# PSUM banks held through the expert stage, skipped parts without zeros, and a nested condition

## The chip, the cores and the metric

The kernel runs on one core of one Trainium2 chip. The metric is the device time of one execution in microseconds (us). Engines are named as in the profile: PE is TensorE (matmuls), PEld its weight loads, DVE is VectorE, ACT is ScalarE, POOL is GpSimd, SP is SyncE, which issues most DMAs. PSUM is the accumulation memory that PE writes and DVE and ACT read; the kernel uses it as eight banks of 128 partitions by 512 float32.

## What is computed

The reference is a two-layer diffusion backbone over 256 latent tokens and 256 context tokens of 1024 features. Each layer mixes tokens (gated linear attention and grouped-query attention in layer 0, Mamba-2 and Fourier mixing in layer 1) and then runs a mixture of 16 experts, of which each token uses two. The change touches only that second half:

```
s = sigmoid(h @ router_w)                      # the two best experts of the best group of four
idx, w = route(h, router_w, router_b)          # w: the two gates, normalised to sum 1
for each expert e, over the tokens x on its list:
    y = (silu(x @ w_gate[e]) * (x @ w_up[e])) @ w_down[e]
    out[token] += gate * y
x = layer_norm(alpha * x + m5 * out)
```

Layer 0 has 512 tokens (context and latent), layer 1 only the 256 latent ones. How many tokens an expert gets is known only at run time.

## The kernel before

The program is straight-line code for each engine; a scheduler with a cost model orders the instructions of each engine when the kernel is built, and semaphores join the engines. In layer 0 the expert stage runs from about 380 to 862 us of the profiled execution, in layer 1 from about 1080 to 1508 us.

*A list in four parts.* The list of an expert has 128 slots, in four parts of 32: part t holds slots 32 t to 32 t + 31. Experts are taken in pairs (members m = 0, even, and m = 1, odd). A part that no token falls into is skipped at run time: `when(rv, least, yes, no)` reads the expert's count from a register and, on PE, compares it with 32, 64 or 96 and branches. Where a part is skipped, the Else branch runs `z_mm` instead: one bf16 matmul of a 128 x 128 tile of zeros (`zero`) that writes zeros over the bank, so that those who read it find numbers. Not every condition has an Else: the combine's second half and the last condition of the down product add to a bank that is already written.

*The steps of a pair*, with the names that the profile uses (0p and 1p stand for the two layers):
- `lists` (sl): the token numbers and gates of the slots, by a matmul of a one-hot matrix G; DVE then copies them out of PSUM into tg, sp, tok and gt (L1508 to L1519). One pair's lists are made while the pair before is computed.
- `features` (xt): the tokens of the slots, features across partitions, in halves S = 0 and S = 1 of 64 slots per member. In layer 0 by an indirect DMA and PE transposes, in layer 1 by a matmul with G. Each half fills two banks, evacuated by ACT. S = 1 is conditional (count over 64).
- `hidden` (gu): gate and up products of the four parts, each in a bank, and `swiglu` by ACT (sg) and DVE (h). Parts 2 and 3 are two conditions, one behind the other.
- `down` (dp): two banks, S = 0 for parts 0 and 1, S = 1 for parts 2 and 3; for S = 1 the product of part 3 stands first with an Else, then that of part 2 without. ACT and DVE take the bank out as y (L316, L1655).
- `combine` (cm): a matmul with one-hot rows adds the pair's outputs at their tokens, and DVE adds the banks to the accumulator, called big (L1562). It runs inside the next pair's odd expert.

*Banks.* `ps(name, tag)` takes a fresh tile out of a pool with three tags: pj (two banks), a (two) and b (four). Each request is a tile of its own, and the pool hands it a bank of its tag as one becomes free in the order that the scheduler settles on. sl, xt and the odd expert's dp use a; the gate and up parts use pj (parts 2 and 3 of even experts b); cm and the even expert's dp use b.

*Helpers.* Every matmul has the line of `mm`, L340, every PE transpose that of `tr`, L345, every condition L1460, and every ACT function L316, so the profile is read by tile names. The weights stream through slots in loads of 1.5 MB on SP's queue.

Of the kernel before, what the change touches and what calls it, by code (L numbers as in the profile page):

```python
# [10 lines left out]
BF16 = mybir.dt.bfloat16  # L11
# [3 lines left out]
OP = mybir.AluOpType  # L15
# [19 lines left out]
# weight slots in the areas while the experts run  # L35
# [3 lines left out]
# ---------------------------------------------------------------- host layout  # L39
# [13 lines left out]
# parameters and constants: '' for the whole run, 'A' and 'B' for the mixers of the two layers  # L53
# [79 lines left out]
def host_layout(a):  # L133
# [41 lines left out]
    # (layer, third, k, half, p, 1024): sixteen units per third, in loads of three and one  # L175
# [19 lines left out]
    # (l, e, k quarter, p, k, tile, gate or up, feature): each tile holds a quarter of the features  # L195
# [3 lines left out]
    # (l, e, half, p, b, output): the partitions hold the b-th 32 features of each quarter  # L199
# [34 lines left out]
# ---------------------------------------------------------------- kernel  # L234

# the column groups of a weight matrix, each loaded where it is first used and kept until it is dropped
# [19 lines left out]
# generators, each a step at a time  # L256
# [6 lines left out]
# pieces of one tile  # L263
# [11 lines left out]
class Core:  # L275
    def __init__(self, tc, I, O, dbg=None, stop=None):
        self.tc, self.nc, self.I, self.O = tc, tc.nc, I, O
        self.dbg, self.stop = dbg or {}, stop
        self.table, self.acts = None, []
        self.held = set()  # L280
        self.pin = False

# [19 lines left out]
    # the four 16 KB areas b, o, a, x hold whatever lives across the parts of a layer  # L302
# [8 lines left out]
    def ps(self, name, tag='a'):  # L311
        return self.psp.tile([128, 512], F32, tag=tag, bufs={'pj': 2, 'a': 2, 'b': 4}[tag], name=name)

    # activations: a table set asked for is loaded behind those that need the one before, and before those that need it
# [62 lines left out]
    # between the layers: LayerNorm, and the modulated input of layer 1  # L377
# [29 lines left out]
    # out = x * exp(-ln(1 + exp(-x))); t is scratch  # L407
# [6 lines left out]
    # a third of layer l's adaLN rows for both streams, as per-partition scalars mods[l][:, m, kt, stream]  # L414
# [57 lines left out]
    # acc = alpha * x + m2 * (o @ w_o); LayerNorm; v = modulated x for the experts; acc = alpha * x  # L472
# [31 lines left out]
    # layer 1's acc = alpha * x + m2 * (o @ w_o), over the features A of o, there before the others, and then B;  # L504
    # of the first N outputs all of A first
# [71 lines left out]
    # out = modulated, and x = alpha * (affine) of the normalized x, the stream h of acc  # L577
# [17 lines left out]
    # rows 0, 1: scale and offset of modulate(n * g + b); rows 2, 3: those of alpha * (n * g + b)  # L595
# [11 lines left out]
    # x (128, KT, n) <- (x - mean) / sqrt(var + eps) over the features, in place  # L607
# [32 lines left out]
    # a stream's LayerNorm, in parts of n tokens, each followed by what is done with it  # L640
# [18 lines left out]
    # scratch of normalize  # L659
# [9 lines left out]
    # x (in place) and its two parts, exact in float32r, of the modulated input  # L669
# [15 lines left out]
    # a weight chunk in two parts  # L685
# [8 lines left out]
    # x in two parts, exact in float32r  # L694
# [9 lines left out]
    # a product of two operands in parts: all but that of the two low parts, which is below float32's accuracy  # L704
# [7 lines left out]
    def even_mixer(self, uT, u, W):  # L712
# [6 lines left out]
        # low-rank decay inputs: partial sums over k on four column tiles  # L719
# [41 lines left out]
        # scratch: the places of the gated linear attention's later results, and the input's  # L761
# [35 lines left out]
    def attention(self, oT, gk, gv):  # L797
        nc, pt = self.nc, self.pt
        # the keys in two parts: the high one of each kv head on both halves of the partitions, the low one where the keys are
# [13 lines left out]
    # 1 / sqrt(scale * x + eps): exp(-ln / 2) and one Newton step y * (1.5 - (scale * x + eps) * y * y / 2)  # L813
# [38 lines left out]
    def gla_states(self, i, q, k_, v, dec, mem):  # L852
# [3 lines left out]
        for di in range(2):  # L856
# [17 lines left out]
            # att[(cp, m), pair, l] = sum_d ke[d, m] qe[d, l], then its causal half  # L874
# [35 lines left out]
    def gla_heads(self, i, S, v, oT, mem):  # L910
        nc = self.nc
        for hh in range(2):
# [14 lines left out]
            # RMS norm over the value features  # L927
# [20 lines left out]
    # heads i (partitions 0-63, kv 0) and i + 4 (partitions 64-127, kv 1)  # L948
    def attend(self, q, k, v, oT, i, strm):
# [4 lines left out]
        # a head's queries in two parts, the high one where they are, the low one on the other half of the partitions  # L954
# [41 lines left out]
    # ------------------------------------------------------------ layer 1 mixer  # L996
# [21 lines left out]
    def odd_mixer(self, uT, parts):  # L1018
# [3 lines left out]
        # by streams: of the context's, nothing is needed once the states are there  # L1022
# [7 lines left out]
        # dt rows: heads of direction 0 at partitions 0-11, of direction 1 at 32-43  # L1030
# [19 lines left out]
        with tc.tile_pool(name='mixB1', bufs=1) as p1:  # L1050
# [17 lines left out]
            # token-major x and b, where the input was  # L1068
# [26 lines left out]
    def dt_tables(self, lr):  # L1095
# [28 lines left out]
        # weights of the tokens in their chunk's final state: dt * exp(sum of the later log decays)  # L1124
# [12 lines left out]
        # decay over the first latent chunk of each direction, on every partition  # L1137
# [38 lines left out]
    def ssd_heads(self, xb, xt, cs, HS, tabs, zs, oT, middle, last):  # L1176
# [4 lines left out]
        # the decays in two parts, exact in float32r, and what picks the rows of both  # L1181
# [266 lines left out]
    def experts(self, l, nb, pm, rows, xg, zero, pos, number, aux):  # L1448
# [4 lines left out]
        def z_mm(p, n):  # L1453
            self.mm(p[:, :n], zero, zero.unsqueeze(1).broadcast_to([128, n // 128, 128]))

        def when(rv, least, yes, no=None):
# [3 lines left out]
            with tc.If(rv > least) as cmp:  # L1460
                yes()
# [305 lines left out]
```

## Time and profile before

| | |
|---|---|
| device time, three runs | 1543.07, 1537.3, 1539.64 us; median 1539.64 |
| span of the profiled execution | 1528.9 us |
| own time of the profiled execution | not listed apart; the median of the runs is 10.7 us above its span |
| PE, DVE, ACT busy | 1298.6, 755.5, 417.4 us |
| mean DMA rate | 260 GB/s |

The span is the time from the first to the last instruction in the trace, the device time also holds what lies around it. "Busy" counts the time in which an engine executes something; matmuls overlap each other, so counts and starts say more about PE than a sum of durations. In an order of events a row is a run of like instructions of one engine: its start, the time to its end, and the count; in square brackets stands how long the engine was idle before it and what it waited for. "issue" means that the engine waited for nothing that the profile shows, "PEq" that PE's own sequencer (branches and semaphores) held it.

### The profile page before, as it was taken

How to read it: one execution, taken by the hardware profiler on the slowest of the kernel's cores; microseconds unless marked ns; L12 is line 12 of the kernel's file. 1: busy time of each engine (PE TensorE's matmuls, PEld its weight loads, DVE VectorE, ACT ScalarE, POOL GpSimd, SP SyncE). 2: the span in 40 equal slices, each digit the busy share in tenths (PEclk: the TensorE clock that was granted, in tenths of full speed). 3: DMA queues.
4: the chain of work that ended last, by engine and by line, in shares of the span. 5: the costliest groups of instructions: out<-in, count | busy, mean ns of one | idle time of the engine just before them, and what ended most of it. 6: DMA issues, size and time to landing. Idle time of an engine off the chain costs nothing. (4 is left out here: it accounts for less than half of the span.)

```text
span 1528.9 us, 28267 instructions
## 1 busy us (share of the span) xinstructions
PE 1298.6 (85%) x11753; PEld 799.5 (52%) x11754; DVE 755.5 (49%) x1899; ACT 417.4 (27%) x831; POOL 66.1 (4%) x68
## 2 busy tenths in 40 slices
PE   3999987996889889999988779989696778987774
PEld 0787643684334454665445348858442455544433
DVE  2756447776426233233344487567541544344534
ACT  3533243452112111111111243444321211121213
POOL 0000002011000000000000030030100000000000
PEclk8999988998899999999999989999898999999876
DMA  9322666044678978779987222652788998999931
GB/s 388 121 93 83 247 249 262 0 172 173 271 304 339 398 300 332 321 293 383 387 359 293 111 85 83 223 204 100 313 321 342 378 373 354 387 375 416 410 129 30
DMA packets 43700, 397.60 MB, mean 260 GB/s; under 512 B 4976, under 2 KB 9200, under 8 KB 12272
## 3 DMA queue, kind: packets, MB, share of 16 engines
q1 hardware_dynamic: 41200, 388.40, 63.1%
q0 software_dynamic: 1728, 4.20, 0.8%
q8 instruction: 158, 2.59, 0.7%
q10 hardware_dynamic: 576, 2.10, 0.3%
q14 instruction: 38, 0.31, 0.1%
HBM read 393.63 MB, written 3.15 MB: 260 GB/s over the span
## 5 line engine op out<-in xcount | busy, mean ns | idle before, releaser
L1599 DVE SCALAR_TENSOR_TENSOR h0p<-gu0p,gt0p,sg0p 128x192 f32<-128x192 f32 x64 | 25.1, 414 | 156.3 <-ACT sg0p L316 155.8
L1599 DVE SCALAR_TENSOR_TENSOR h1p<-gu1p,gt1p,sg1p 128x192 f32<-128x192 f32 x64 | 26.5, 414 | 142.2 <-ACT sg1p L316 142.2
L340 PE MATMUL gu1p<-more,big 128*32 128x384 f32 x976 | 87.2, 497 | 8.9 <-issue 5.1
L340 PE MATMUL gu0p<-big,xe0p 128*32 128x384 f32 x992 | 92.5, 494 | 0.2 <-DVE h0p L1599 0.2
L316 ACT ACTIVATE sg0p<-gu0p 128x192 f32<-128x192 f32 x64 | 19.7, 332 | 215.0 <-PE gu0p L340 211.8
L316 ACT ACTIVATE y0p<-dp0p 64x512 fp32r<-64x512 f32 x64 | 37.9, 591 | 147.9 <-PE dp0p L340 105.0
L340 PE MATMUL gu0p<-ring,xe0p 128*32 128x384 f32 x768 | 75.1, 490 | 1.5 <-ACT sg0p L316 0.8
L340 PE MATMUL gu0p<-more,xe0p 128*32 128x384 f32 x800 | 73.7, 488 | 0.9 <-issue 0.9
L1655 DVE TENSOR_TENSOR y0p<-dp0p,y0p 64x512 fp32r<-64x512 f32 x64 | 44.0, 688 | 58.2 <-ACT y0p L316 57.6
L340 PE MATMUL ada<-ring,small 128*32 128x512 f32 x344 | 60.1, 641 | 14.4 <-DMA ring<-in_ada 14.4
L316 ACT ACTIVATE sg1p<-gu1p 128x192 f32<-128x192 f32 x64 | 21.2, 330 | 183.5 <-PE gu1p L340 159.9
L340 PE MATMUL dp0p<-big,hT0p 128*32 128x256 f32 x792 | 59.6, 390 | 8.7 <-issue 6.1
L340 PEld LDWEIGHTS gu1p<-more,big 128*32 128x32 f32 x976 | 39.5, 112 | 51.6 <-issue 37.8
L1655 DVE TENSOR_TENSOR y1p<-dp1p,y1p 64x512 fp32r<-64x512 f32 x64 | 44.0, 688 | 42.9 <-ACT y1p L316 40.2
L340 PEld LDWEIGHTS gu0p<-big,xe0p 128*32 128x32 f32 x992 | 47.9, 111 | 32.9 <-issue 20.3
L316 ACT ACTIVATE y1p<-dp1p 64x512 fp32r<-64x512 f32 x64 | 37.8, 591 | 93.0 <-PE dp1p L340 49.1
L1562 DVE SCALAR_TENSOR_TENSOR big<-cm0p,mods,big 128x256 f32<-128x256 f32 x128 | 51.6, 476 | 20.0 <-PEq L1460 10.0
L340 PE MATMUL gu1p<-big 128*32 128x384 f32 x528 | 54.5, 521 | 4.0 <-issue 4.0
L340 PE MATMUL cm0p<-oh0p,y0p 128*128 128x512 f32 x192 | 55.2, 417 | 2.7 <-DVE big L1562 1.2
L316 ACT ACTIVATE big<-big 128x512 f32<-128x512 f32 (+2 forms) x81 | 44.7, 575 | 46.7 <-DVE big L626 19.4
L340 PE MATMUL zo<-zo,zw 128*128 128x256 f32 x384 | 54.6, 292 | 0.0
L340 PEld LDWEIGHTS zo<-zo,zw 128*128 128x128 f32 x384 | 48.6, 191 | 6.6 <-issue 4.3
(537 smaller groups left out, 2483.8 us busy)
## 6 DMA issues: line engine op xcount, KB each, us to landing
more<-in_egu SPq DMA_DIRECT2D x54, 1536.0 KB, 11.1
big<-in_egu SPq DMA_DIRECT2D x48, 1536.0 KB, 13.9
ring<-in_ada SPq DMA_DIRECT2D x27, 1536.0 KB, 7.3
ring<-in_ed SPq DMA_DIRECT2D x27, 1536.0 KB, 9.4
ring<-in_egu SPq DMA_DIRECT2D x26, 1536.0 KB, 10.1
big<-in_ed SPq DMA_DIRECT2D x21, 1536.0 KB, 10.6
more<-in_ed SPq DMA_DIRECT2D x16, 1536.0 KB, 10.6
ring<-in_odw SPq DMA_DIRECT2D x5, 1536.0 KB, 7.5
```

What stands on the lines that cost most here:

```text
L316: a = self.nc.scalar.activation(out, x, func, **kw)
L340: i = self.nc.tensor.matmul(out, lhsT, rhs, start=start, stop=stop, skip_group_check=True)
L1562: nc.vector.scalar_tensor_tensor(self.acc[:, h, f], y, self.mods[l][:, 5, f, h:h + 1], self.acc[:, h, f], op0=OP.mult, op1=OP.add)
L1599: nc.vector.scalar_tensor_tensor(H[:, t], p[:, 192:384], gt[:, 2 * m + t % 2, i, t // 2:t // 2 + 1], sg, op0=OP.mult, op1=OP.mult)
L1655: nc.vector.tensor_tensor(yl[r], dp[r], yh[r].bitcast(F32), op=OP.subtract)
```

## The change

Four things change.

1. `open_banks(l)` takes eight tiles, one per bank, at the start of the expert stage and keeps them to its end. Each is written with zeros once. Inside the stage `ps` hands these tiles out in turn for each tag, in the order in which the program is written, not in the order in which they become free.
2. The Else branches and `z_mm` are gone. A skipped part leaves in its bank what was there: finite numbers, which are multiplied by a gate of zero or by empty one-hot rows. What PE does on the false side is only the semaphore update that the others count on.
3. Part 3's condition stands inside part 2's in `hidden`, and the same in `down` for S = 1. For S = 0 of `down`, part 0's product stands before part 1's.
4. The tile of zeros is a piece of a tile of the routing (r2) instead of one of its own. Comments are removed; L340 becomes L354, L345 L359, L1460 L1471.

```diff
@@ class Core @@
+    def open_banks(self, l):
+        zero = self.zero
+        self.nc.vector.tensor_scalar(zero, self.C('ident'), 0.0, None, op0=OP.mult)
+        banks = {tag: [self.ps(f'bank{l}{tag}{i}', tag) for i in range(n)] for tag, n in (('pj', 2), ('a', 2), ('b', 4))}
+        for b in banks['pj'] + banks['b'] + banks['a']:
+            self.mm(b, zero, zero.unsqueeze(1).broadcast_to([128, 4, 128]))
+        self.banks = banks
...
     def ps(self, name, tag='a'):
+        if self.banks:
+            b = self.banks[tag]
+            b.append(b.pop(0))
+            return b[-1]
         return self.psp.tile([128, 512], F32, tag=tag, bufs={'pj': 2, 'a': 2, 'b': 4}[tag], name=name)
...
@@ moe @@
-            zero = self.pm.tile([128, 128], BF16, name=f'zero{l}')
-            nc.vector.tensor_scalar(zero, self.C('ident'), 0.0, None, op0=OP.mult)
+            self.zero = r2[:, 704:768].bitcast(BF16)
...
@@ experts @@
-        def z_mm(p, n):
-            self.mm(p[:, :n], zero, zero.unsqueeze(1).broadcast_to([128, n // 128, 128]))
-
-        def when(rv, least, yes, no=None):
+        def when(rv, least, yes):
...
-            with tc.If(rv > least) as cmp:
+            with tc.If(rv > least):
                 yes()
-            if no:
-                with cmp.Else():
-                    no()
...
@@ features @@
-                    when(rv, 64, t_mm, lambda: [z_mm(p[c], 512) for c in range(2)])
+                    when(rv, 64, t_mm)
...
@@ hidden @@
-            def part(t, j=range(4)):
-                p = self.ps(f'gu{l}{nm}{t}', 'pj' if m or t < 2 else 'b')
-                when(rv if t > l_first else None, 32 * t, lambda: [gu_mm(t, jj, p) for jj in j], lambda: z_mm(p, 384))
-                return p
-            l_first = 0 if l else 1
+            def psum(t):
+                return self.ps(f'gu{l}{nm}{t}', 'pj' if m or t < 2 else 'b')
+
+            def part(t):
+                for j in range(4):
+                    gu_mm(t, j, p[t])
+            p = [psum(t) for t in range(2)]
             if l:
-                p = [part(0)]
+                part(0)
                 middle()
-                p.append(part(1))
+                when(rv, 32, lambda: part(1))
...
             between()
+            p += [psum(t) for t in (2, 3)]
+
+            def more():
+                part(2)
+                when(rv, 96, lambda: part(3))
+            when(rv, 64, more)
             for t in (2, 3):
-                swiglu(t, part(t))
+                swiglu(t, p[t])
...
@@ down @@
                 if S == 0:
-                    if l:
-                        when(rv, 32, lambda: d_mm(1), lambda: z_mm(dp, 512))
-                    else:
-                        d_mm(1)
                     d_mm(0)
+                    when(rv if l else None, 32, lambda: d_mm(1))
                 else:
-                    when(rv, 96, lambda: d_mm(1), lambda: z_mm(dp, 512))
-                    when(rv, 64, lambda: d_mm(0))
+                    def more():
+                        d_mm(0)
+                        when(rv, 96, lambda: d_mm(1))
+                    when(rv, 64, more)
...
@@ the expert stage @@
         cnt, nwin = self.counts(l, number)
+        self.open_banks(l)
...
         self.dump(f'acc{l}', self.acc.rearrange('p h k t -> p (h k t)'))
+        self.banks = None
```

What this does to the order of PE's program is shown at three places. In the rows, a name's last digits before the underscore are the bank's number (bank1a1: layer 1, tag a, number 1) or the pair, member and half.

PE in layer 0, the down product of the first odd expert, before: one condition with its Else, five matmuls, another condition.

```order
L1460 COMPARE_AND_BRANCH
L340 MATMUL dp0p111_4575<-ring_64,hT0p11_4405 32x256 x12
L340 MATMUL dp0p111_4575<-big_63,hT0p11_4405 32x256 x12
L1460 UNCONDITIONAL_BRANCH
L340 LDWEIGHTS zero0_2766
L340 MATMUL dp0p111_4575<-zero0_2766 128x512
L1460 UNCONDITIONAL_BRANCH
L340 MATMUL dp0p110_4522<-big_63,hT0p11_4405 32x256 x5
L1460 COMPARE_AND_BRANCH
L340 MATMUL dp0p111_4575<-ring_64,hT0p11_4405 32x256 x12
```

The same product after:

```order
L1471 COMPARE_AND_BRANCH
L354 MATMUL bank0a1_2912<-ring_64,hT0p11_4357 32x256 x12
L354 MATMUL bank0a1_2912<-big_63,hT0p11_4357 32x256 x12
L1471 COMPARE_AND_BRANCH
L354 MATMUL bank0a1_2912<-ring_64,hT0p11_4357 32x256 x12
L354 MATMUL bank0a1_2912<-big_63,hT0p11_4357 32x256 x12
L1471 UNCONDITIONAL_BRANCH x3
L354 MATMUL bank0a0_2911<-big_63,hT0p11_4357 32x256 x12
```

The second condition now stands inside the first one's body, behind part 2's product, and is only met where the first holds; both join at the three branches behind it. The zero and its Else are gone.

PE in layer 1, the lists of the next pair (sl1p2), the first half of its gather (xt1p200 is that half's first bank) and the combine of the pair before (cm1p01), before:

```order
L340 MATMUL sl1p2_12407<-aux1_11157,small_65 128x8 x4
L340 MATMUL xt1p200_12465<-small_65,xg10_11071 128x128
L340 MATMUL xt1p200_12465<-small_65,xg11_11072 128x128
L340 MATMUL cm1p011_12307<-oh1p002_12273,y1p0010_11768 128x256
L340 MATMUL cm1p011_12307<-oh1p002_12273,y1p0011_11769 128x256
L340 MATMUL xt1p200_12465<-small_65,xg10_11071 128x128
L340 MATMUL cm1p012_12308<-oh1p003_12277,y1p0010_11768 128x256
L340 MATMUL cm1p012_12308<-oh1p003_12277,y1p0011_11769 128x256
L340 MATMUL xt1p200_12465<-small_65,xg11_11072 128x128
L340 MATMUL cm1p013_12309<-oh1p003_12277,y1p0010_11768 128x256
L340 MATMUL cm1p013_12309<-oh1p003_12277,y1p0011_11769 128x256
L1460 COMPARE_AND_BRANCH
```

The same place a pair later, after (banks by name: bank1a1 takes sl, bank1b0 to b3 the combine, and the bank1a1 matmuls behind it are the gather's second bank):

```order
L354 MATMUL bank1a1_11033<-aux1_10885,small_65 128x8 x4
L354 MATMUL bank1b3_11037<-oh1p202_13385,y1p2010_12898 128x256
L354 MATMUL bank1b3_11037<-oh1p202_13385,y1p2011_12899 128x256
L354 MATMUL bank1b0_11034<-oh1p203_13389,y1p2010_12898 128x256
L354 MATMUL bank1b0_11034<-oh1p203_13389,y1p2011_12899 128x256
L354 MATMUL bank1b1_11035<-oh1p203_13389,y1p2010_12898 128x256
L354 MATMUL bank1b1_11035<-oh1p203_13389,y1p2011_12899 128x256
L1471 COMPARE_AND_BRANCH
...
L354 MATMUL bank1a1_11033<-small_65,xg10_10801 128x128
L354 MATMUL bank1a1_11033<-small_65,xg11_10802 128x128
...
L1471 COMPARE_AND_BRANCH
```

The matmuls of the gather's first bank no longer stand between the combine's; the second bank's stand behind the combine's last condition and write the bank that the lists were written to. The first bank's matmuls now stand ahead of the odd expert's first part, still on PE:

```order
L1471 UNCONDITIONAL_BRANCH x2
L354 MATMUL bank1a0_11032<-small_65,xg10_10801 128x128
L354 MATMUL bank1a0_11032<-small_65,xg11_10802 128x128
...
L354 MATMUL bank1pj0_11030<-more12_10799,big_63 32x384 x8
L354 MATMUL bank1pj0_11030<-more13_10800,big_63 32x384 x16
L1471 COMPARE_AND_BRANCH
```

They have moved up by one odd expert's gate and up products.

DVE at that place, after: who reads bank1a1 (lists), and what stands ahead of it.

```order
L1570 SCALAR_TENSOR_TENSOR big_63<-bank1b2_11036,mods1_77,big_63 128x256
L1570 SCALAR_TENSOR_TENSOR big_63<-bank1b3_11037,mods1_77,big_63 128x256
L1570 SCALAR_TENSOR_TENSOR big_63<-bank1b0_11034,mods1_77,big_63 128x256
L1570 SCALAR_TENSOR_TENSOR big_63<-bank1b1_11035,mods1_77,big_63 128x256
L1607 SCALAR_TENSOR_TENSOR h1p31_13370<-bank1pj1_11031,gt1p3_12817,sg1p313_13504 128x192
L1516 COPY tg1p4_13513<-bank1a1_11033 64x2
L1517 COPY sp1p4_13514<-bank1a1_11033 64x2
...
L1518 TENSOR_TENSOR tg1p4_13513<-sp1p4_13514,bank1a1_11033 64x2
L1516 COPY tg1p4_13513<-bank1a1_11033 64x2
...
L1518 TENSOR_TENSOR tg1p4_13513<-sp1p4_13514,bank1a1_11033 64x2
```

The last reader of the lists in bank1a1 is the TENSOR_TENSOR that closes the fence; it stands behind the combine's four adds and one swiglu product.

## Rows read from the trace of the kernel before

**Rows 1.** The page's head and its first part: engine, busy us, share, instructions.
```profile
span 1528.9 us, 28267 instructions
...
PE 1298.6 (85%) x11753; PEld 799.5 (52%) x11754; DVE 755.5 (49%) x1899; ACT 417.4 (27%) x831; POOL 66.1 (4%) x68
```

**Rows 2.** Windows, PE alone: stretch, length, busy, clock, DMA share, GB/s.
```profile
380.00:862.00 482.00, 437.60 (x4943) 0.97 0.78 316
1080.00:1508.00 428.00, 333.76 (x3537) 0.90 0.81 333
```

**Rows 3.** Instructions reading the tile zero: duration ns min/median/max, first and last start.
```profile
L340 PE MATMUL gu1p<-zero x38: 322/337/525, 1105.6 to 1479.3; 128*128 128x384 bf16 x38
L340 PE MATMUL gu0p<-zero x24: 322/325/499, 400.1 to 818.4; 128*128 128x384 bf16 x24
L340 PE MATMUL dp1p<-zero x23: 379/391/634, 1122.4 to 1494.8; 128*128 128x512 bf16 x23
L340 PE MATMUL dp0p<-zero x14: 377/390/391, 428.9 to 840.0; 128*128 128x512 bf16 x14
L340 PE MATMUL xt1p<-zero x14: 376/379/390, 1105.8 to 1440.3; 128*128 128x512 bf16 x14
L340 PE MATMUL xt0p<-zero x8: 376/380/390, 427.8 to 771.8; 128*128 128x512 bf16 x8
```

**Rows 4.** Order of events on PE, layer 0, a down product with two skips.
```profile
574.00 1.67 PE L340 MATMUL dp0p<-big,hT0p 128*32 128x256 f32 x24
575.60 0.39 PE L340 MATMUL dp0p<-zero 128*128 128x512 bf16 x1
575.92 1.05 PE L340 MATMUL dp0p<-big,hT0p 128*32 128x256 f32 x10
577.12 1.24 PE L340 MATMUL dp0p<-big,hT0p 128*32 128x256 f32 x17
```

**Rows 5.** Order of events on PE, layer 0, a zero between combine matmuls.
```profile
598.21 1.20 PE L340 MATMUL cm0p<-oh0p,y0p 128*128 128x512 f32 x4
599.36 0.32 PE L340 MATMUL gu0p<-zero 128*128 128x384 bf16 x1
599.39 1.22 PE L340 MATMUL cm0p<-oh0p,y0p 128*128 128x512 f32 x4
```

**Rows 6.** PE's waits, 1104 to 1506 us: us in total, times, longest.
```profile
PE gu1p L340 <- issue: 25.7, 10, 5.0
PE dp1p L340 <- issue: 18.1, 8, 4.7
PE dp1p L340 <- PEq L1460: 13.6, 8, 5.3
PE xt1p L340 <- ACT big L316: 6.5, 11, 0.7
```

**Rows 7.** Order of events on PE, layer 1, end of a combine and the gather.
```profile
1188.31 0.48 PE L340 MATMUL cm1p<-oh1p,y1p 128*128 128x256 f32 x2
1188.94 1.13 PE L340 MATMUL xt1p<-small,xg 128*128 128x128 f32 x8
1190.76 2.05 PE L340 MATMUL xt1p<-small,xg 128*128 128x128 f32 x16 [0.69 <-ACT big L316]
1192.65 0.38 PE L340 MATMUL xt1p<-zero 128*128 128x512 bf16 x1
1193.49 0.38 PE L340 MATMUL xt1p<-zero 128*128 128x512 bf16 x1 [0.47 <-ACT big L316]
```

**Rows 8.** Order of events on DVE at the same place.
```profile
1188.92 1.66 DVE L1562 SCALAR_TENSOR_TENSOR big<-cm1p,mods,big 128x256 f32<-128x256 f32 x4 [1.74 <-PEq L1460]
...
1192.16 0.16 DVE L1510 TENSOR_TENSOR tg1p<-sp1p,sl1p 64x2 f32<-64x2 f32 x1
```

**Rows 9.** Order of events on PE, layer 1, two stalls behind skipped parts.
```profile
1208.38 0.50 PE L340 MATMUL gu1p<-zero 128*128 128x384 bf16 x1 [4.21 <-issue]
...
1246.88 2.80 PE L340 MATMUL dp1p<-ring,hT1p 128*32 128x256 f32 x48 [2.48 <-PEq L1460]
```

More of the change, by code (lines that the diff above doesn't have):

```diff
@@ L1411, in moe @@
                 self.store(l, j)
-            self.experts(l, nb, pm, self.rows, self.xg, zero, *lists)
+            self.experts(l, nb, pm, self.rows, self.xg, *lists)
         self.slots = [i for i in self.slots if i in self.ring1]
@@ L1446, in spare, with experts @@
         return self.big[:, 12288 + 1024 * i:13312 + 1024 * i]
-    def experts(self, l, nb, pm, rows, xg, zero, pos, number, aux):
+    def experts(self, l, nb, pm, rows, xg, pos, number, aux):
         nc, tc = self.nc, self.tc
@@ L1599, in swiglu @@
                 nc.vector.scalar_tensor_tensor(H[:, t], p[:, 192:384], gt[:, 2 * m + t % 2, i, t // 2:t // 2 + 1], sg, op0=OP.mult, op1=OP.mult)
-            def part(t, j=range(4)):
-                p = self.ps(f'gu{l}{nm}{t}', 'pj' if m or t < 2 else 'b')
-                when(rv if t > l_first else None, 32 * t, lambda: [gu_mm(t, jj, p) for jj in j], lambda: z_mm(p, 384))
-                return p
-            l_first = 0 if l else 1
+            def psum(t):
[4 more added lines that the diff above has]
+            p = [psum(t) for t in range(2)]
             if l:
-                p = [part(0)]
+                part(0)
                 middle()
-                p.append(part(1))
+                when(rv, 32, lambda: part(1))
             else:
-                p = [self.ps(f'gu{l}{nm}{t}', 'pj') for t in range(2)]
                 for j in range(4):
@@ L1748, in experts @@
                     combine('w', Y, tok, 0, None)
+        self.banks = None
         self.dump(f'acc{l}', self.acc.rearrange('p h k t -> p (h k t)'))
```

## The prediction

> **What bounds the kernel now.** The summary page comes first: TensorE (PE) is busy 1298.6 of a span of 1528.9 us [rows 1], no other engine above half, so only what PE executes or waits for counts. The median of the runs shown, 1539.64 us, is 10.7 us above that span; the profiled execution's own time is taken as its span plus these 10.7 us. The change touches nothing but the two expert stages, so the next view is the busy time of those two stretches [rows 2]. In layer 0's (380 to 862 us) PE works 437.6 of 482 us at a granted clock of 0.97: what is taken from PE's program there shortens the kernel nearly one for one. In layer 1's (1080 to 1508 us) it works 333.8 of 428 us at 0.90, so 94 us are waits, and a shorter program need not be a shorter stage. The view of waits tells which: of layer 1's, 25.7 and 18.1 us are "issue" in front of gate/up (gu1p) and down (dp1p) matmuls and 13.6 us PE's sequencer (PEq) in front of dp1p [rows 6], 57.4 us in 26 waits. The order of events shows where these sit: behind skipped parts, 4.21 us in front of a zero matmul at 1208.38, 2.48 us at 1246.88 where a jump precedes dp1p [rows 9]. PE waits there for its own instructions, not for data. Weights hardly ever bind.
>
> **What the change removes.** The matmuls that read the tile of zeros count the skipped parts [rows 3]. Layer 0: gu0p 24, dp0p 14, xt0p 8. So 14 experts have at most 96 tokens and 10 of them at most 64 (14 + 10 = 24), and four pairs skip the second half of the gather. Layer 1: gu1p 38 (16 + 15 + 7 with at most 96, 64 and 32), dp1p 23 (16 + 7), xt1p 14, which is seven pairs. In all 121 zero matmuls.
>
> *Price of one skip.* At 574.00 twenty-four dp0p begin, at a pitch of 54 ns (last start 1.29 us after the first: 1.67 less one matmul of 0.38). The next real one would start at 575.30; it starts at 575.92, so a skip with a zero matmul costs 0.62, less than 0.05 of which is pitch: 0.57 us. The ten matmuls from 575.92 take 0.74 us at their pitch, and the next group starts at 577.12, behind a skip without a zero (the last condition of the down product never had one): 0.46 us [rows 4]. The zero itself is thus worth 0.1 us, and the condition 0.46 us that stay. What pays is the nesting: where the third part is skipped, the fourth's condition is not even met, and a whole skip goes. The zero can also be free: between combine matmuls at 598.21 to 600.61, eight of them at 0.29 us each fill the time, and the zero at 599.36 adds under 0.1 us [rows 5].
>
> *Layer 0.* Down: 10 experts lose one whole skip, 10 x 0.57 = 5.7 us, and 4 only the zero, 4 x 0.1: 6.1 us. Gate/up: of the 10 experts that skip both parts, the gain is between 0.1 (the second of two neighbouring zeros hid already) and 0.6 us; I take 0.2, since the second of neighbours has its branch decided under the first: 2.0 us. Against it three odd experts that compute part three and skip part four had their zero hidden between combine matmuls (under 0.1 us) and now meet a bare skip of 0.46: -1.2 us. Gather: four pairs of zeros become one skip each; between 0 and 0.75 us, I take 0.3: 1.2 us. Sum 8.1, of which 7.5 us are taken to reach the end, since PE is nearly full there.
>
> *Layer 1.* Down: 15 nests x 0.4 to 0.57 us; the three conditions stand side by side before, so I take 0.4: 6 us. Gather: the two zeros hold PE from 1192.65 to 1193.87, 0.47 of it a wait for ScalarE (ACT) [rows 7]; one bare skip is left: 1.2 - 0.46, of which I take 0.6, x 7 = 4 us. Gate/up: 16 x 0.2 = 3 us. Sum 13 us. Of it I let 3 us disappear in the fetch stalls above (bounds 0 and 13): a PE that arrives earlier at a jump whose target isn't there waits longer.
>
> *What it adds in layer 1: a wait.* Banks are now handed out in program order. Tag "a" has two, and a pair uses them seven times: lists, two halves of the first gather, two of the second, two down products. The lists' bank and that of the gather's second half are therefore the same one (bank1a1 in the rows of the order), and the second half must wait until VectorE (DVE) has read the lists for the last time. Before, the second half took the bank that came free first, and waited 0.69 us for ACT's evacuation of the first half, 11 such waits and 6.5 us in the stage [rows 6, 7]. DVE is in order, and in front of the lists it has the four combine adds: they begin at 1188.92 (behind the last combine matmul, 1188.79), and the last read of the lists runs at 1192.16 for 0.16 us [rows 8]. So the second half could start at 1192.32, 3.5 us after the combine, where before it started at 1190.76, and of those 1.97 us 1.13 were matmuls of the first half, which now run ahead of the odd expert's first part. Idle time grows from 0.84 to 3.53: 2.7 us x 7 pairs = 18.9 us. Behind the waiting matmul stand the down product of the even expert and the next gate/up products; everything on PE follows it. Bounds: 0, if DVE were done earlier, and 3.5 x 7 = 24.5.
>
> *Given back.* While PE waits there, its next instructions can arrive. Stalls that stood shortly behind the place (2.48 us at 1246.88 [rows 9], and others of its kind) would shrink: bounds 0 and 18.9; I take 9, three to four such places at 2.5 us.
>
> The Trainium skill, "Runtime: NRT & Kernel Launch", section "Instruction fetch mechanics", says that a taken branch whose target lies outside the pages already fetched stalls until that page arrives. By that rule the nest speaks against itself: one jump over two bodies reaches twice as far as either did. The stalls in front of a zero in the rows agree with the rule; it would make the nest worth less than a skip in layer 1, and it is the second rival.
>
> *Start of the stage.* Eight zero matmuls per layer, 0.4 us each by the 0.39 us of a 512-column one [rows 3], 6.4 us in all, but in the routing, where PE waits for DVE; 0.5 us taken (bounds 0 and 6.4).
>
> **Sum.** Layer 0 -7.5; layer 1 -13 + 3 + 18.9 - 9 = 0; start +0.5. In all -7 us: 1528.9 - 7 = 1521.9 of span, and with the 10.7 around it 1532.6, forecast 1533 us.
>
> **Rivals.** First, the wait is not there or hides wholly in the fetch stalls, and what was cut lands: -7.5 - 13 + 0.5 = -20, or -14 if a part is swallowed: 1520 to 1526, say 1522. For it speaks that 57 us of PE's waits are of a kind that time heals; against it that the wait comes at a place where only part of the pairs have a stall behind it. Second, jumps: the longer jumps of the nests miss their code more often, layer 1 gives back its gain and layer 0 half of its own: -3 us or so, 1537. For it, the 4.21 us behind one skip; against it, that the code fetched in total does not grow. Third, slower: the lists' bank. All of the 18.9 us land, none given back, and layer 1's gain of 13 goes into fetch stalls: -7.5 + 18.9 + 0.5 = +12, 1552 us. For it speaks that DVE's row of adds and reads lies in full behind the combine; against it that the stage's fetch stalls then can't be as long as before. It decides once a pair loses over 2 us net in layer 1. Fourth, that the change does not do what it says can hardly be: the zeros are gone from the order.
>
> **Numbers.** A difference of 0.5% (7.7 us) is about what a measurement of this kernel can tell from none. Forecast case 0.50, spread 1525 to 1541, nearly half of it below 1532. First rival 0.20, all faster; second 0.12, all but a little within 0.5%; third 0.18, slower. Faster 0.22 + 0.20 = 0.42; same 0.27 + 0.11 = 0.38; slower 0.20. The range takes the first rival's centre less its spread and reaches to the third's centre: 1516 to 1553; the forecast case alone, 1525 to 1541.
>
> **What would show it.** In the profile after, no tile of zeros inside the stages; PE's busy time down by about 40 us of zeros (121 x 0.35), most of which overlapped others. Layer 0's stage shorter by 7 to 8 us. In layer 1, seven waits of PE for DVE's reads of the lists in front of the gather's second half, 2 to 3.5 us each, and fewer issue waits in front of dp1p. Wrong would be: no such wait; stalls at nests that were not there before; layer 0 not shorter.

## The result, and the profile after

The changed kernel takes 1554.31 us (median of 9 runs, 1543.63 to 1556.4), the kernel before 1540.03 in the same session. The ratio is 1.0069, 95% interval [1.0045, 1.0092]: slower by 0.7%, where 0.4% faster was forecast; 1.3 us above the range, on the side and next to the number of the third rival (1552). The profile is of the slowest of the nine, that of the kernel before was of an execution shorter than all its timed ones.

The page's head and first part, and windows over the two expert stages (stretch, length, PE busy, granted clock, DMA share, GB/s):

```profile
span 1554.6 us, 27956 instructions
...
PE 1304.7 (84%) x11648; PEld 805.8 (52%) x11649; DVE 756.8 (49%) x1899; ACT 417.3 (27%) x831; POOL 66.1 (4%) x68
```
```profile
384.00:870.00 486.00, 431.59 (x4900) 0.96 0.78 313
1091.00:1534.00 443.00, 339.51 (x3472) 0.86 0.79 323
```

Against [rows 1, 2] PE executes less and is not busy for less time, and layer 1's clock is lower, 0.86 for 0.90. No skipped part reads a tile of zeros any more. From the last matmul of the routing (pos) to the end of the stage, layer 0 takes 487.4 us for 484.0 before, layer 1 427.2 for 412.7. The rest of the profiles' difference of 25.7 us lies outside the stages; device times differ by 14.3. The windows of layer 0's stage, before and after:

```profile
378.40:862.40 484.00, 438.15 (x4953) 0.97 0.78 314
```
```profile
382.80:870.20 487.40, 431.96 (x4910) 0.95 0.77 312
```

Layer 1's waits of PE, and the events around one of the first kind on PE and on DVE:

```profile
PE bank1pj L354 <- PEq L1471: 22.0, 14, 5.0
PE bank1a L354 <- DVE tg1p L1518: 21.0, 7, 3.6
PE bank1a L354 <- PEq L1471: 12.8, 10, 4.4
PE bank1a L354 <- issue: 8.9, 6, 3.4
```
```profile
1200.65 0.96 PE L354 MATMUL bank1b<-oh1p,y1p 128*128 128x256 f32 x6
1205.19 4.25 PE L354 MATMUL bank1a<-small,xg 128*128 128x128 f32 x16 [3.58 <-DVE tg1p L1518]
1209.59 0.63 PE L354 MATMUL bank1b<-ring,hT1p 128*32 128x256 f32 x4
```
```profile
1201.74 1.66 DVE L1570 SCALAR_TENSOR_TENSOR big<-bank1b,mods,big 128x256 f32<-128x256 f32 x4 [0.85 <-PEq L1471]
...
1204.98 0.16 DVE L1518 TENSOR_TENSOR tg1p<-sp1p,bank1a 64x2 f32<-64x2 f32 x1
```

The wait stands where it was expected, seven times, up to 3.6 us: 21.0 us in all, where ACT's 6.5 us stood in [rows 6, 7]. What was not expected is the second row's length: the same sixteen matmuls took 2.05 us in [rows 7] and take 4.25 here, at the lower level of the clock (granted 0.5 from 1202.46 to 1209.29).

In layer 0, a down product behind its nest (answering [rows 4]) and the place behind a skipped gate/up nest:

```profile
576.52 1.98 PE L354 MATMUL bank0pj<-big,xe0p 128*32 128x384 f32 x18
578.12 5.91 PE L354 MATMUL bank0a<-big,hT0p 128*32 128x256 f32 x96
...
692.10 2.79 PE L354 MATMUL bank0pj<-ring,xe0p 128*32 128x384 f32 x32
697.30 3.42 PE L354 MATMUL bank0pj<-more,xe0p 128*32 128x384 f32 x20 [2.41 <-PEq L1471]
```

At 697.30 PE had waited 2.41 us for its own sequencer, and twenty matmuls then took 3.42 us, where 32 take 2.79 at the full clock.

**Where layer 1's time went.** Two sums over the trace show it. The granted clock is recorded in stretches; PE's busy time inside those at the lower level (1.2 GHz), halved, is what it would be at the upper one (2.4). And PE's branch instructions carry their durations; "late code" below is what those over 0.7 us last beyond 0.3 us. Idle is the stage less PE's busy time.

| us | before, two profiles | after |
|---|---|---|
| layer 0: stage | 484.0, 488.8 | 487.4 |
| PE busy, recalculated to the upper level | 430.4, 430.3 | 415.0 |
| busy at the lower level | 15.4, 18.5 | 34.0 |
| PE idle | 45.9, 49.3 | 55.4 |
| late code | 13.7, 13.8 | 24.7 |
| layer 1: stage | 412.7, 413.6 | 427.2 |
| PE busy, recalculated | 298.3, 299.1 | 284.0 |
| busy at the lower level | 51.8, 59.4 | 88.3 |
| PE idle | 88.4, 84.9 | 99.0 |
| late code | 47.0, 50.1 | 44.1 |

PE's work at the upper level is 15 us less in each layer. In layer 1 the lower clock takes 16 of them back ((88.3 - 55.6) / 2), and 12 us of idle time come on top: +14. In layer 0 clock (8 us) and idle time (8 us) cancel the 15.

### The profile page after: what moved, and what is told of

The parts are those of the page before. It is cut to its first block, busy times and chain, and to the rows that moved or that the text cites. A ratio compares the mean times of both kernels' runs of the same rounds, so it can differ in the third digit from the quotient of the medians.

```text
span 1554.6 us, 27956 instructions
## 1 busy us (share of the span) xinstructions
PE 1304.7 (84%) x11648; PEld 805.8 (52%) x11649; DVE 756.8 (49%) x1899; ACT 417.3 (27%) x831; POOL 66.1 (4%) x68
## 5 line engine op out<-in xcount | busy, mean ns | idle before, releaser
L354 PE MATMUL bank1pj<-more,big 128*32 128x384 f32 x976 | 86.9, 503 | 10.1 <-issue 5.2
L354 PE MATMUL bank0pj<-big,xe0p 128*32 128x384 f32 x832 | 76.3, 494 | 0.2 <-DVE h0p L1607 0.2
L1570 DVE SCALAR_TENSOR_TENSOR big<-bank0b,mods,big 128x256 f32<-128x256 f32 x128 | 51.6, 477 | 41.4 <-PEq L1471 23.3
L354 PE MATMUL bank0pj<-more,xe0p 128*32 128x384 f32 x752 | 69.3, 497 | 2.9 <-PEq L1471 2.6
L354 PE MATMUL ada<-ring,small 128*32 128x512 f32 x320 | 58.7, 678 | 13.7 <-DMA ring<-in_ada 13.6
L354 PE MATMUL bank1a<-small,xg 128*128 128x128 f32 x256 | 46.8, 351 | 26.9 <-DVE tg1p L1518 20.7
L354 PE MATMUL bank1pj<-big 128*32 128x384 f32 x528 | 54.0, 526 | 17.2 <-PEq L1471 16.3
L354 PE MATMUL bank0pj<-ring,xe0p 128*32 128x384 f32 x656 | 63.7, 491 | 5.2 <-PEq L1471 2.7
L354 PE MATMUL bank0b<-oh0p,y0p 128*128 128x512 f32 x192 | 57.4, 421 | 11.5 <-PEq L1471 4.5
L354 PEld LDWEIGHTS bank1pj<-more,big 128*32 128x32 f32 x976 | 34.7, 113 | 57.0 <-issue 53.3
L354 PEld LDWEIGHTS bank1a<-small,xg 128*128 128x128 f32 x256 | 42.1, 255 | 34.7 <-DVE tg1p L1518 23.1
L330 ACT ACTIVATE big<-big 128x512 f32<-128x512 f32 (+2 forms) x81 | 44.7, 575 | 49.3 <-DVE big L640 22.0
L354 PE MATMUL zo<-zo,zw 128*128 128x256 f32 x384 | 56.2, 297 | 0.0
L354 PEld LDWEIGHTS zo<-zo,zw 128*128 128x128 f32 x384 | 50.1, 197 | 6.6 <-issue 4.3
L354 PEld LDWEIGHTS bank0pj<-big,xe0p 128*32 128x32 f32 x832 | 37.1, 111 | 30.8 <-issue 25.8
L354 PEld LDWEIGHTS bank0b<-oh0p,y0p 128*128 128x128 f32 x192 | 32.5, 188 | 38.9 <-issue 15.8
L330 ACT ACTIVATE y0p<-bank0b 64x512 fp32r<-64x512 f32 x32 | 18.9, 592 | 114.6 <-PE bank0b L354 72.3
L354 PE MATMUL bank1b<-ring,hT1p 128*32 128x256 f32 x528 | 40.3, 449 | 10.7 <-PEq L1471 5.2
```

Source lines behind the costliest of these rows:

```text
L330: a = self.nc.scalar.activation(out, x, func, **kw)
L354: i = self.nc.tensor.matmul(out, lhsT, rhs, start=start, stop=stop, skip_group_check=True)
L1570: nc.vector.scalar_tensor_tensor(self.acc[:, h, f], y, self.mods[l][:, 5, f, h:h + 1], self.acc[:, h, f], op0=OP.mult, op1=OP.add)
```

## The experiments

Each ratio is to the kernel before in its own session. All are whole kernels unless it is said what is left out.

**Parts of the change alone.** Four versions: one bank for layer 1's first gather; no nest; the nest alone; the kept banks alone.

```diff
 # e1_list_bank: features, layer 1, S = 0
-                p = [self.ps(f'xt{l}{nm}{S}{c}') for c in range(2)]
+                p = [self.ps(f'xt{l}{nm}{S}')] * 2      # evacuated between the halves
 # e2_no_nest
-            when(rv, 64, more)
+            when(rv, 64, lambda: part(2)); when(rv, 96, lambda: part(3))
 # e3_nest_only: the kernel before, with
+            when(rv, 64, third, lambda: [z_mm(x, 384) for x in q])   # third holds when(rv, 96, ...)
 # e4_banks_only: the changed kernel, not nested, every when(...) with its z_mm
```

> The changed kernel, but in layer 1 both halves of the first gather go through one bank, with the evacuation between them, so that the lists' bank is no longer written by the gather. Bank theory (the changed kernel is slower because PE waits 7 x 3.6 us for DVE's reads of the lists, and works at half clock behind each wait): the seven waits are gone, 21 us and the slow matmuls behind them, less some 5 us of fetch stalls that come back; about 1530 to 1535 us, ratio to the kernel before 0.993 to 0.998. Jump theory (the nests' longer jumps cost instruction fetches): the waits go but turn into fetch stalls, 1548 to 1555 us, ratio 1.005 to 1.01.

> The changed kernel with the two conditions one behind the other as before, banks kept and no zeros. Bank theory: the seven waits of 3.6 us stay, and each of 10 + 15 skipped pairs in the down products and some of the gate/up ones cost a bare skip of 0.46 us more: 1554 to 1566 us, ratio 1.009 to 1.017. Jump theory: the stalls at the nests go, layer 0 gets 8 us shorter than in the changed kernel; 1540 to 1546 us, ratio 1.00 to 1.004.

> The kernel before with the nest alone: banks as they come free, zeros written where parts are skipped (the outer Else writes for both). Bank theory: no wait for the lists, a whole skip less at 25 down products: 1530 to 1537 us, ratio 0.993 to 0.998. Jump theory: the nests bring the stalls, 1545 us or more, ratio 1.003 to 1.01.

> The kernel before with the kept banks alone, handed out in program order; zeros and separate conditions as before. Bank theory: seven waits for DVE's reads of the lists, and nothing saved: 1555 to 1570 us, ratio 1.01 to 1.02. Jump theory: as before, 1537 to 1543 us, ratio 0.998 to 1.002.

Measured: e1 1551.87 us, ratio 1.0071 [1.0042, 1.0099]; e2 1563.89, 1.0141 [1.0100, 1.0181]; e3 1555.75, 1.0097 [1.0059, 1.0135]; e4 1549.12, 1.0048 [1.0024, 1.0072]. The nest alone (e3) and the kept banks alone (e4) are each slower than before, and mending the bank gains nothing. By their numbers e1 and e3 fell to the jump theory, e2 to the bank theory, and e4 lies in neither range, so neither theory holds for all four. PE's waits in layer 1 of e1:

```profile
PE bank1a L354 <- issue: 21.9, 10, 3.2
PE bank1pj L354 <- PEq L1471: 20.5, 12, 4.7
PE bank1b L354 <- PEq L1471: 19.4, 9, 4.2
...
PE bank1a L354 <- DVE tg1p L1518: 3.5, 1, 3.5
```

The bank's waits fell from 21.0 to 3.5 us, and waits for "issue" and PEq rose from 59.0 to 81.2: all of it came back as waits for code (late code as defined above: 44.1 to 60.3). The stage stayed at 427.3 us. So the waits alone are not shown to be the loss. But each of these versions also puts its code at other places, which is worth as much (below), and none of them settles its part by itself.

**Is it the weights' traffic?** The kernel before again for a second profile, and kernels before and after with quarter loads in layer 1 (outputs of layer 1 then use old weights).

```diff
-        d = self.nc.sync.dma_start(t[:, :n], src)
+        r = 32 if slot already loaded in layer 1 else 128
+        d = self.nc.sync.dma_start(t[:r, :n], src[:r])
```

> The kernel before, unchanged, for a second profile, since its first profiled execution was shorter than all its timed ones. If the stages vary by instruction fetch, layer 1's stage differs from the first profile's by 5 to 15 us and all of it is in stalls behind branches, at the same busy time; if not, it repeats within 3 us.

> The kernel before, but in layer 1's expert stage each weight slot is loaded whole only the first time and by a quarter (32 of 128 partitions) afterwards: the DMA traffic there drops to about a third, the instructions of all engines stay. Fetch theory (instructions come late because their packets queue among those of the weights): layer 1's stall behind branches falls from 47 to under 15 us and the kernel gets 30 us shorter or more. Rival (a fetch takes its time whatever the traffic): the stalls stay at 40 us or more, the time within 8 us.

> The changed kernel with the same quarter loads in layer 1's expert stage. Fetch theory: with instructions there in time the waits of the lists' bank count in full and so do the skips saved, so it is between 5 us longer and 5 us shorter than the kernel before with quarter loads, with 7 waits of about 3.5 us for DVE. Rival: as slow against it as with whole loads, 12 to 15 us.

Measured: b2 1537.45 us with a span of 1535.4, so some 2 us lie around a span, and the 10.7 of the prediction were mostly a fast profiled execution; its layer 1 repeats within 1 us (413.6). f1 1528.15, ratio 0.9911 [0.9878, 0.9943]; f2 1547.87, 1.0039 [1.0021, 1.0056]. With the one bank as well (f3_thin_list_bank): 1552.7, 1.0063 [1.0042, 1.0085]. With quarter loads the changed kernel is 20 us slower than the one before, more than either theory had, and the one bank made it no faster, where the fetch theory had 12 us. The windows row of f1's layer 1:

```profile
1104.90:1508.70 403.80, 322.23 (x3491) 0.91 0.40 89
```

Traffic fell from 328 to 89 GB/s, and late code stayed (46.6 us for 47.0), though the stage is 9 us shorter and the kernel 13, more than the rival's 8. In the changed kernel (f2) late code fell, from 44.1 to 32.1 us, but PE's idle time did not (100.9 for 99.0). In the kernel before the weights' traffic is not the cause of late code; my fetch theory in that form fell.

**Length of the code.** Both kernels, and the changed one with one bank, without the code of the fourth part in layer 1, which no list there enters (what is left out otherwise are its conditions); and the nest dropped, wholly or in gate/up alone.

```diff
 # g1, g3: in layer 1            # g2: in layer 1
-  when(rv, 96, ...)            -  when(rv, 96, ..., lambda: z_mm(...))
                                +  z_mm(...)
 # e5: e1 and e2 together; h1: e1, with gate/up as in e2 and down nested
```

> The changed kernel without the code of the fourth part in layer 1 (no list there is longer than 96, so nothing that runs is left out but 16 conditions inside nests never entered but once): 14.4 blocks of 256 instructions less. Fetch-pitch theory: layer 1's stage is shorter by 14 x 3 us or more, its stalls behind branches under 25 us; 1505 to 1520 us. If the fetch of code has no part in it: within 5 us of the changed kernel.

> The kernel before without the code and conditions of the fourth part in layer 1, its zeros written always: 14.4 blocks of instructions less. Fetch-pitch theory: 25 to 45 us shorter than before, 1495 to 1515 us, and the changed kernel without that code is 8 to 15 us slower than this one, by the waits of the lists' bank that no fetch hides now. Otherwise within 8 us of before.

> The changed kernel with one bank for the first gather and without the code of the fourth part in layer 1 (nothing that runs is left out but its conditions). With 14 blocks of code less, fetches no longer take up what the waits of the lists' bank release: fetch-pitch theory: 10 to 20 us shorter than the same without the one bank, 1484 to 1494 us, level with or under the kernel before without that code (1491.8). If code arriving has nothing to do with it: the same as without the one bank, 1500 to 1506 us.

> The changed kernel with one bank for layer 1's first gather and with the conditions of parts three and four one behind the other (no nest at all), no zeros. Long-jump theory (a nest's jump over 261 or more instruction slots lands beyond what has been fetched ahead, and that eats what the change saves): layer 0's stalls behind branches come back to 12 to 15 us from 27, layer 1's to about 50 from 60; 1540 to 1546 us. Fetch-pitch theory (layer 1 streams 66 to 69 blocks of 256 instructions at 6 us each, so what is taken away turns into stalls): as the version with the nest and the one bank, 1549 to 1556 us.

> As the changed kernel with one bank for layer 1's first gather, but the nest only in the down products (jumps of 197 slots), gate/up conditions one behind the other (131 each). Long-jump theory: layer 0's stalls fall to 12 to 15 us, its stage to about 478 us, layer 1's stage to 415 to 420; 1533 to 1540 us. Fetch-pitch theory: layer 1's stage stays at 427, layer 0's falls; about 1545 us.

Measured: g1 1503.69 us, ratio 0.9736 [0.9705, 0.9767]; g2 1491.82, 0.9665 [0.9635, 0.9695]; g3 1489.71, 0.9666 [0.9648, 0.9684]; e5 1553.56, 1.0068 [1.0050, 1.0087]; h1 1553.25, 1.0070 [1.0046, 1.0095]. The instruction queue of the page, after and in g1 (packets, MB, share of 16 engines):

```profile
q8 instruction: 157, 2.57, 0.7%
```
```profile
q8 instruction: 143, 2.34, 0.6%
```

14.4 x 256 instruction slots less are 14 packets less, of 16 KB each. Code that is jumped over is fetched all the same. Its removal is worth 51 us in g1, 49 in g2 and 62 in g3 against e1, 3.5 to 4.4 us a packet, the largest effect of the study. g1 is the plain case, since PE meets only two branches fewer in layer 1 (112 for 114); in g2 it meets 32 fewer. The jumps get shorter too and all later code moves, and how much of the gain is due to that was not separated. Layer 1's windows of g1, g2, g3:

```profile
1107.80:1490.40 382.60, 311.04 (x3414) 0.89 0.85 353
```
```profile
1103.90:1473.60 369.70, 312.39 (x3487) 0.95 0.88 365
```
```profile
1103.90:1469.70 365.80, 303.58 (x3414) 0.93 0.89 369
```

With short code the lists' bank seems to count: g1 is 12 us slower than g2, and the one bank (g3) takes 14 us off it, which with long code gave nothing; each was run in one placement only. e5 lies where the fetch-pitch theory had it, h1 in neither range: without the gate/up nest layer 0's late code came back from 27.0 to 15.6 and 13.5 us, but neither total moved from e1's. In the changed kernel's layer 0, of the ten gate/up skips behind a jump of 261 to 263 slots, six stall over 0.7 us, 23.7 us in all; of the 24 conditions of 131 slots before, four, 10.8 us. Yet with zeros in place the same nest left layer 0's late code at 13.8 (e3) and 15.3 us (k2), so the length of the jump alone is not shown to be the cause.

The Trainium skill, "Runtime: NRT & Kernel Launch", section "Instruction fetch mechanics", says of these 16 KiB blocks of 256 instructions that crossing one is mostly hidden, and that a taken branch whose target is outside the current pages stalls. The rows agree with the second: the 47 us of late code in layer 1 before stand at branches. Whether crossings without a jump are hidden no run here shows.

**Is it the clock?** Eight zero matmuls in each wait for the lists; and zeros on every skip with nest and one bank.

```diff
 # k3: combine, layer 1, behind the adds
+                        for _ in range(2): self.mm(ps[dd], zero, ...)
 # k2: e1, each when(...) with its z_mm again
```

> The changed kernel with eight zero matmuls per pair in layer 1, into the combine's four banks behind the adds that read them, where PE waits for DVE's reads of the lists; the waits' length stays. Clock theory (the bare skips and the waits let the granted clock fall to its lower level, and the work behind them takes twice as long): the sixteen gather matmuls behind each wait take 2 us instead of 4.25, the work at the lower level in layer 1 falls from 88 us to 65 or less, and the kernel is 8 to 14 us shorter than the changed one: 1540 to 1546 us. Fetch-pitch theory alone (time in layer 1 is set by when code arrives): no gain, 1551 to 1558 us.

> The changed kernel with one bank for layer 1's first gather and a zero matmul again where a part is skipped (nest kept, the outer false side writes both banks). Clock theory: the zeros hold the clock, work at the lower level falls from 81 to about 60 us in layer 1 and from 34 to about 16 in layer 0, which pays for the zeros' own 15 us in each: within 5 us of the version without them (1547 to 1557 us). If the clock has no part in it: the zeros cost their 15 to 25 us, 1565 us or more.

Measured: k3 1558.24 us, ratio 1.0120 [1.0101, 1.0139]; k2 1548.97, 1.0059 [1.0039, 1.0079]. The same place in k3:

```profile
1195.73 3.38 PE L354 MATMUL bank1b<-zero 128*128 128x512 bf16 x8 [0.67 <-DVE big L1570]
1198.95 1.50 PE L354 MATMUL bank1a<-small,xg 128*128 128x128 f32 x12
1200.60 0.68 PE L354 MATMUL bank1a<-small,xg 128*128 128x128 f32 x4
1205.84 6.94 PE L354 MATMUL bank1b<-ring,hT1p 128*32 128x256 f32 x96 [4.55 <-PEq L1471]
```

There the sixteen matmuls take 2.2 us, at a granted clock of 1.0 where it was 0.5: with the gap filled PE had its upper clock there. But work at the lower level fell only to 79 us, and the next row waits 4.55 us for code: at this place, what the clock gave, the fetch took. k2's time landed where the clock theory had it, and in layer 0 work at the lower level fell from 34 to 22.5 us; in layer 1 it did not fall (82.2 for 80.5, where 60 was expected), and the lists' waits returned in its order (20.3 us), so it separates little.

**Where the code lies.** 32 matmuls (128 slots) in code of layer 0 that is jumped over; nothing more is executed, and the order is the same.

```diff
         with tc.If(most > 128):
+            if l == 0:
+                for _ in range(32):
+                    self.mm(bank[:, :128], self.C('ident'), self.C('ident'))
```

> The kernel before with 32 matmuls (128 instruction slots) added to code of layer 0 that is jumped over, so that all of layer 1's code on PE lies half a block of 256 slots later; nothing more is executed. If the kernel before owes its short layer 1 (413 us against 420 to 438 in all versions whose code lies elsewhere) to where its jumps fall against blocks: layer 1's stage 418 to 432 us, 1546 to 1558 us. If not: within 3 us of before.

> The changed kernel with the same 128 slots ahead of layer 1. If the place of the code decides: layer 1's stage moves by 5 us or more either way, with its stalls behind branches, at the same seven waits of 3.6 us. If not: within 3 us of the changed kernel.

Measured: m1 1556.9 us, ratio 1.0105 [1.0071, 1.0140]; m2 1530.62, 0.9930 [0.9906, 0.9955]. Half a block turns the verdict round. Counted along layer 1's branches, all 18 that last over 0.7 us in the kernel before do so again in its second profile (20 there); m1 has 26, and shares one of the 18. m2 has 23, and shares 10 of the changed kernel's 17. Layer 1's windows of the kernel before, m1, the changed kernel, m2:

```profile
1097.40:1510.00 412.60, 324.19 (x3487) 0.91 0.80 328
```
```profile
1106.10:1531.50 425.40, 331.83 (x3488) 0.91 0.78 319
```
```profile
1108.90:1536.10 427.20, 328.19 (x3418) 0.87 0.78 317
```
```profile
1103.10:1512.90 409.80, 312.89 (x3418) 0.88 0.81 330
```

m2 keeps the waits for the lists:

```profile
PE bank1a L354 <- DVE tg1p L1518: 20.8, 8, 3.6
```

It has even more late code (56.0 us for 44.1), but it falls elsewhere: work at the lower clock is 65 us for 88, which is 11.5 of the 15 us by which PE is busy for less. m1 has 66.1 us of late code for 47.0. By these profiles the change costs layer 1 14.5 us in one placement, against a kernel before in a good one, and gains 15.6 in the other (425.4 to 409.8); by device time it costs 14.3 and gains 26.3.

**A version that is faster than both.** By its ratio m2 is. So, less, is banks kept in layer 0 alone, with zeros and no nest.

```diff
 # k1: e4, and
-        self.open_banks(l)
+        if l == 0:
+            self.open_banks(l)
```

> The kernel before with banks kept in layer 0 alone (zeros and separate conditions as before), since with banks kept and zeros in both layers layer 0's stage was 477 us against 484 to 489. If that was the banks: layer 0's stage 476 to 481 us, layer 1's 411 to 418, 1530 to 1535 us, a version faster than both. If it was where the jumps fell against what had been fetched: layer 0's stage 483 us or more and no gain, 1538 to 1546 us.

Measured: 1538.61 us, ratio 0.9969 [0.9948, 0.9990]; layer 0 in 478.7 us as expected, layer 1 in 419.9 with late code of 64.2. The window of its layer 0:

```profile
378.70:857.40 478.70, 437.52 (x4956) 0.97 0.78 318
```

That gain repeats: layer 0 takes 477.4 us in e4, which has the same layer 0, and 484.0 to 488.8 in five profiles with the kernel before's. After m1 and m2, it can't be put down to banks: the code of both layers also lies elsewhere.

## Why the prediction was wrong

1. *What is saved.* PE's work at the upper clock fell by 15 us in each layer, 30 us where about 40 us of zeros were named. That is not the quantity that was summed: 8.1 and 13 us were times of skips, which no row measures apart. PE's busy time as recorded did not fall.
2. *The step that failed* is the one from work to time: "7.5 us are taken to reach the end, since PE is nearly full there" and, in layer 1, "of it I let 3 us disappear in the fetch stalls". In layer 0 nothing reached the end: five profiles with the kernel before's layer 0 average 487.1 us, seven with the changed one's 487.3 (484.6 to 489.1). Layer 1 grew by 14 us as the two kernels were placed. The sum priced what remains at the durations of before and had no term for the clock. But PE was idle for 8 us more in layer 0 and 12 in layer 1, and more of its work ran at the lower clock: 8 us in layer 0 and 16 in layer 1. Layer 0 had 11 us more of late code too, which stood among the rivals and not in the sum. Of the prediction's own signs of being wrong, two came: layer 0 not shorter, and stalls at nests. The zeros seem to have held part of this off: with banks kept and zeros (e4, k1, k2) layer 0 takes 477.4 to 480.2 us with 14 to 23 us of work at the lower clock, without zeros in every version 484.6 to 489.1 with 25 to 38. The place of the code was not held fixed between these.
3. *The lists' bank.* Seven waits, 3.6 us at most, in the place forecast. Their 21.0 us stand against seven times 3.53, 24.7; less the seven times 0.84 that stood there before, about 15 us came on, for 18.9. They aren't shown to be the loss: taken away (e1), the time is the same, and m2 is faster than the kernel before with all of them.
4. *Given back.* 9 us were taken; late code fell by 3 to 6 us in the changed kernel. That it would refill what a mended wait releases (e1, 17.5 us for 22) is the same exchange seen from the other side, and there it was complete.
5. *The rivals.* The third named the wait, the number and the side; its mechanism may explain the time with short code (g1 against g2 and g3), but isn't shown for this one, so the nearness of its 1552 is luck. The second had layer 1 give back its gain and layer 0 half of its own; both gave back all, and the sign was wrong.
6. *What no case had:* the verdict hangs on where layer 1's code begins. Over the two placements tried the kernel before averages 1549 us (1541.3, 1556.9) and the changed one 1542 (1554.3, 1530.6). That this is near the 7 us forecast is luck as far as is known: the forecast took them from layer 0, which is no shorter, and in the profiles layer 1 averages 419.0 us before and 418.5 after. Two placements are too few to call it a gain. How placement decides which jumps wait, and so where the clock falls, stays open.

## What to carry to other kernels

Where PE waits for "issue" or PEq behind branches, count the code that is jumped over too: it is fetched, and leaving it out was worth more than any instruction saved on the path. In such a stage a change of about 1% can't be judged from one build: here half a fetch block was worth 1.0 and 1.5%. Move the code by that much with instructions that are never executed, in both kernels, before believing either sign. And price work behind a new gap at both levels of the clock.

## What was not expected of the hardware

- A shift of 128 instruction slots in code that never runs moved one program by +16 us and the other by -24.
- Quarter weight loads, 89 for 328 GB/s, left late code at 46.6 us for 47.0 in the kernel before.
- Eight bf16 matmuls of zeros in a gap of 3.6 us made the sixteen float32 ones behind it take 2.2 us for 4.25.
